# A two-layer decoder trunk on one core: the FFN's gate and up product as seven half-size products in place of eight

## The chip, the core and the metric

The kernel runs on one core of a Trainium2 chip: TensorE (PE) for matrix products, VectorE (DVE), ScalarE (ACT) and GpSimd (POOL) for elementwise work, SyncE (SP) for issuing transfers. The metric is the device time of one launch, in microseconds; lower is better.

## The reference

Two layers, each of them FFN, mixer, FFN, over 512 tokens of width 1024; the mixer of layer 0 is sparse attention over selected keys, that of layer 1 a gated spatial mixer. Only the FFN is touched by the change. It is run four times, with weights of its own each time:

```python
D_MODEL = 1024; SEQ = 512; D_FF = 2816
def swiglu(x, w_in, w_out):
    gate, up = jnp.split(x @ w_in, 2, axis=-1)
    return (jax.nn.silu(gate) * up) @ w_out
...
    h = x
    for i in range(DEPTH):
        h = h + 0.5 * swiglu(rmsnorm(h, norm_g[i, 0]), ffn_w_in[i, 0], ffn_w_out[i, 0])
        hn = rmsnorm(h, norm_g[i, 1])
        y = mixer_a(...) if kind == 0 else mixer_b(...)
        h = h + y
        h = h + 0.5 * swiglu(rmsnorm(h, norm_g[i, 2]), ffn_w_in[i, 1], ffn_w_out[i, 1])
    return rmsnorm(h, final_g)
```

## The kernel before

**Layout.** The residual stream stays in SBUF as eight tiles `H[j]` of 128 features x 512 tokens, features on the partitions. `weigh` (L177 to L180) turns each into two fp32r parts: `XH[j]` is the tile times the norm's gain, rounded, and `XL[j]` what the rounding left. The row scale of the norm is applied behind the product, since it depends on the token alone. Every weight tile of 128x128 is split in the same way into `whi` and `wlo`. `mul3` (L219 to L224) makes one product of full precision from three matmuls: whi by XH, whi by XL, wlo by XH, each with 512 columns. A product of one k tile is thus three matmuls and three weight loads.

**The weight stream.** All weights come in one order, written out by hand: `in_wst` holds them eight tiles to a load of 512 KB. `WeightStream` (L54) loads them on the SP queue into four `raw` buffers (L74), splits four tiles at a time (ACT makes `whi`, L91; DVE, in some stages POOL, makes `wlo`, L92) into six pairs of buffers, and `take` hands them to the next product. Each engine executes in the order in which the code is written, so a row that waits holds all rows behind it on its engine.

**The FFN** (`ffn`, L247). w_in has 22 gate tiles and 22 up tiles of output columns. The first four (gate 0, up 0, gate 1, up 1) are made together in four PSUM banks, k by k, in `group` (L230), so that they can start while the tiles of `XH` are still being made; all others one after the other, eight k each, in `single` (L240). `token_scale` (L198) makes the row scale with two matmuls against ones. `activate` (L256 to L268) multiplies gate and up by the row scale, applies silu and splits the result into `yh` and `yl`. When 11 of the 22 are there, their share of the product with w_out is made, and `scalar_tensor_tensor` at L318 adds half of it to `H[j]`. That is done twice; in the last FFN the second time in two halves of 256 tokens (`parts=2`), so that the final norm of one half can run beside the products of the other. `finish` starts the next stage's `weigh` and square sum as soon as a tile of `H` is complete. In the first FFN the `weigh` of tile k+1 and the square sum run in hooks behind k (`behind`), and a table of biases for the mixer, `dist`, is written to DRAM behind k = 3 (L345).

## Time and profile before

| what | value |
|---|---|
| median of 3 runs | 2143.5 us (2143.36 to 2143.62) |
| the profiled execution | 2143.43 us |
| its span, first to last instruction | 2141.7 us |
| PE busy | 2122.9 us, 9816 matmuls |
| PE weight loads busy | 1768.2 us |
| DVE busy | 1141.6 us |
| ACT busy | 752.7 us |
| POOL busy | 131.7 us |
| mean DMA rate | 100 GB/s |

Busy time is printed from the start of an instruction to its modelled end. Matmuls are pipelined: a matmul begins before the printed end of the one in front, and the distance between two starts tells what one costs in a row of them. An engine's share of the span is an average over stages; the rows by window and the timeline show a stage by itself.

### The profile page before, as it was taken

To read this page: it belongs to the slowest core of one execution; us is meant where nothing else is said; L and a number is where in the kernel's file an instruction comes from. 1 tells how busy PE (TensorE), PEld (TensorE's weight loads), DVE (VectorE), ACT (ScalarE), POOL (GpSimd) and SP (SyncE) were. 2 spreads that over 40 slices of the span, in tenths; PEclk is the share of its full clock that TensorE was granted. 3 is DMA by queue.
4 is the path that set the end of the run, shared out by engine and by line. 5 is a ranking of instruction groups with operands and counts; after the bars stand their busy time and mean duration, and the time that the engine had idled before them with its cause. 6 is when DMAs were issued, how large, how long until landed. Compare 5 with 4: busy or idle time off the path is not lost.

```text
span 2141.7 us, 25553 instructions
## 1 busy us (share of the span) xinstructions
PE 2122.9 (99%) x9816; PEld 1768.2 (83%) x9816; DVE 1141.6 (53%) x1968; ACT 752.7 (35%) x1317; POOL 131.7 (6%) x122
## 2 busy tenths in 40 slices
PE   8999999999999999999999999999999999999998
...
GB/s 182 134 99 99 94 93 99 88 105 83 61 89 99 98 99 93 95 88 108 99 98 93 95 99 89 149 88 90 97 91 94 86 89 104 99 99 94 94 127 129
DMA packets 60426, 214.67 MB, mean 100 GB/s; under 512 B 7232, under 2 KB 8320, under 8 KB 60176
## 3 DMA queue, kind: packets, MB, share of 16 engines
...
## 4 chain that ended last, share of the span: by engine, by line
PE 95%; DMA 3%; issue 1%; POOL 1%; DVE 0%; ACT 0%; POOLq 0%; ACTq 0%
PE acc L222 16%; PE acc L223 16%; PE acc L224 16%; PE aux L224 12%; PE aux L222 12%; PE aux L223 12%; DMA raw<-in_wst 2%; PE aux L648 1%; PE acc L647 1%; PE aux L647 1%; PE acc L648 1%; PE aux L646 1%; PE acc L646 1%; PE aux L698 1%; PE acc L565 1%
## 5 line engine op out<-in xcount | busy, mean ns | idle before, releaser
L91 ACT ACTIVATE whi<-raw 128x512 fp32r<-128x512 f32 x768 | 466.5, 625 | 743.6 <-PE acc L223 351.5
L92 DVE TENSOR_TENSOR wlo<-raw,whi 128x512 fp32r<-128x512 f32 x698 | 474.8, 701 | 445.4 <-ACT whi L91 445.1
L222 PE MATMUL acc<-xh,whi 128*128 128x512 f32 x1048 | 418.1, 399 | 6.4 <-ACT xh L179 5.5
L224 PE MATMUL acc<-xh,wlo 128*128 128x512 f32 x1048 | 409.0, 390 | 0.6 <-POOL wlo L92 0.6
L223 PE MATMUL acc<-xl,whi 128*128 128x512 f32 x1048 | 409.0, 390 | 0.0
L222 PE MATMUL aux<-xh,whi 128*128 128x512 f32 x720 | 280.2, 389 | 1.0 <-ACT whi L91 1.0
L224 PE MATMUL aux<-xh,wlo 128*128 128x512 f32 x720 | 280.2, 389 | 0.6 <-POOL wlo L92 0.6
L223 PE MATMUL aux<-xl,whi 128*128 128x512 f32 x720 | 280.1, 389 | 0.0
L222 PEld LDWEIGHTS acc<-xh,whi 128*128 128x128 f32 x1048 | 197.4, 188 | 49.0 <-ACT xh L179 5.5
L224 PEld LDWEIGHTS acc<-xh,wlo 128*128 128x128 f32 x1048 | 197.1, 188 | 42.5 <-POOL wlo L92 1.1
L223 PEld LDWEIGHTS acc<-xl,whi 128*128 128x128 f32 x1048 | 197.4, 188 | 41.9 <-issue 1.4
L222 PEld LDWEIGHTS aux<-xh,whi 128*128 128x128 f32 x720 | 135.1, 188 | 29.4 <-ACT whi L91 1.4
L224 PEld LDWEIGHTS aux<-xh,wlo 128*128 128x128 f32 x720 | 135.1, 188 | 29.2 <-POOL wlo L92 1.1
L223 PEld LDWEIGHTS aux<-xl,whi 128*128 128x128 f32 x720 | 135.1, 188 | 28.0
L222 PE MATMUL aux<-yh,whi 128*128 128x512 f32 (+1 forms) x396 | 144.8, 366 | 0.0
L222 PE MATMUL acc<-yh,whi 128*128 128x512 f32 (+1 forms) x396 | 144.8, 366 | 0.0
L223 PE MATMUL aux<-yl,whi 128*128 128x512 f32 (+1 forms) x396 | 144.7, 365 | 0.0
L224 PE MATMUL aux<-yh,wlo 128*128 128x512 f32 (+1 forms) x396 | 144.7, 365 | 0.0
L223 PE MATMUL acc<-yl,whi 128*128 128x512 f32 (+1 forms) x396 | 144.7, 365 | 0.0
L224 PE MATMUL acc<-yh,wlo 128*128 128x512 f32 (+1 forms) x396 | 144.7, 365 | 0.0
L92 POOL TENSOR_TENSOR wlo<-raw,whi 128x512 fp32r<-128x512 f32 x70 | 93.3, 1346 | 166.3 <-ACT whi L91 114.6
L245 DVE TENSOR_TENSOR yl<-a,yh 128x512 fp32r<-128x512 f32 x88 | 62.5, 711 | 61.5 <-ACT yh L244 61.5
...
## 6 DMA issues: line engine op xcount, KB each, us to landing
raw<-in_wst SPq DMA_DIRECT2D x383, 512.0 KB, 3.5
dist<-rows POOLq DMA_DIRECT2D x1, 2560.0 KB, 56.8
...
wT<-in_wspT POOLq DMA_DIRECT2D x1, 512.0 KB, 8.3
```

Source lines behind the costliest of these rows:

```text
L91: self.nc.scalar.activation(hi, src, AF.Copy)
L92: self.lo_engine.tensor_tensor(lo, src, hi.bitcast(F32), op=ALU.subtract)
L222: mm(ps, wh, xh, start=first, stop=False)
L223: mm(ps, wh, xl, start=False, stop=False)
L224: mm(ps, wl, xh, start=False, stop=last)
L245: nc.vector.tensor_tensor(lo, src, hi.bitcast(F32), op=ALU.subtract)
L565: mm(po[0][:, b * P:(b + 1) * P], V[j][:, h * P:(h + 1) * P], pT[:, j * P:(j + 1) * P], start=j == 0, stop=j == b)
L646: mm(banks[t], xh, wh, start=k == 0, stop=False)
L647: mm(banks[t], xl, wh, start=False, stop=False)
L648: mm(banks[t], xh, wl, start=False, stop=k == KD - 1)
L698: mm(ps[:, t * P:(t + 1) * P], V[t][:, d * P:(d + 1) * P], wT[:, g, :], start=True, stop=True)
```

## The change

Gate and up tiles 0 and 1 stay as they are, in `group`. The other 20 pairs are taken two at a time, ten double pairs for each FFN: two gate tiles and the two up tiles beside them. For such a double pair the sum over k is cut in two (even and odd k tiles) and the tokens in two (`n1`, the first 256, and `n2`). The product of a 2x2 arrangement of weights (gate and up by even and odd k) with a 2x2 arrangement of operands (even and odd k by first and second half) is then made with seven products in place of eight, by Winograd's form of Strassen's scheme.

- `sums(kp)` makes the four sums of operands that are needed, for each of four pairs of k tiles: ACT scales two tiles of `H` by the gain, POOL makes four differences, ACT and DVE split them into `TH[kp]` and `TL[kp]`. It is called in `group`'s hooks behind k = 1, 3, 5, 7.
- `_source` makes the weights of the seven products ("forms") from four loads r11, r21, r22, r12 (gate by even k, up by even k, up by odd k, gate by odd k): forms 0, 3 and 6 are loads as they are, forms 1, 2, 4 and 5 are DVE sums. Each form is eight weight tiles, and ACT and DVE split it in instructions of 1024 columns.
- `two_pairs` issues the seven products, each 2 x 4 x 3 matmuls of 256 columns, into three PSUM banks A, B, C. ACT copies intermediate results out of PSUM (m1, m5, u2, u3), DVE and POOL add them, POOL multiplies the gate by the row scale, and silu, the product and the split into `yl` are spread over the next products by `later` and `step`.
- `WeightStream` works in units of eight tiles in place of four. Plain units ("P") are split into three buffers `w`, forms ("F") into these or two more, `x`; forms are only made inside an FFN. Of the loads, r22 has a single buffer of its own.
- The output product is made in three chunks (3, 4 and 3 double pairs; 8, 8 and 6 k tiles) in place of two halves of 11, the first four `H` tiles together, the others one by one. In front of silu only the gate is multiplied by the row scale; for the up half it is applied here, times 1/2 (`rh`), so that `H[j]` takes two DVE instructions in place of one.
- The row scale is made from four columns (`scale_columns`, `scale_rows`) with fp32 matmuls. In the last stage the output is scaled in place in `H`, and each tile has a transfer of its own in place of one for two tiles.

```diff
+CHUNKS = (3, 4, 3)
+FFN_PLAN = "PPPP" + "SSS" + "P" * 8 + "SSSS" + "P" * 8 + "SSS" + "P" * 6
+PLAN = FFN_PLAN + "P" * 37 + FFN_PLAN + FFN_PLAN + "P" * 72 + FFN_PLAN + "P" * 6
+N_LOADS = sum(4 if k == "S" else 1 for k in PLAN)
...
+    RINGS = {"raw": 4, "r22": 1, "w": 3, "x": 2}
+    FORMS = 7
...
+                self.loads += [("raw", base + 4), ("raw", base + 4), ("r22", base + 6), ("raw", base + 5)]
+                self.units += [("F", n, f) for f in range(self.FORMS)]
...
+    def _free(self, ring, below):
+        used, n = self.used[ring], self.RINGS[ring]
+        return len(used) < n or used[-n] < below
...
+    def _split(self, src, hi, lo, s=slice(0, LOAD * P)):
+        self.nc.scalar.activation(hi[:, s], src[:, s], AF.Copy)
+        self.lo_engine.tensor_tensor(lo[:, s], src[:, s], hi[:, s].bitcast(F32), op=ALU.subtract)
...
+    def _source(self, i, f):
+        r11, r21, r22, r12 = (self.raw.get(i + j) for j in range(4))
+        tt = self.nc.vector.tensor_tensor
+        if f == 0:
+            return r11
+        if f == 1:
+            self.sum = self.spool.tile([P, LOAD * P], F32, tag="wsum", bufs=1, name=f"wsum{i}")
+            tt(self.sum, r21, r22, op=ALU.add)
+            return self.sum
+        if f == 2:
+            tt(self.sum, self.sum, r11, op=ALU.subtract)
+            return self.sum
+        if f == 3:
+            return r12
+        if f == 4:
+            tt(r21, r11, r21, op=ALU.subtract)
+            return r21
+        if f == 5:
+            tt(r12, r12, self.sum, op=ALU.subtract)
+            return r12
+        return r22
...
+            if kind == "F" and self.spool is None:
+                break
+            self._load_to(self.loaded + 4)
+            rings = [r for r in ("w", "x")[:1 if kind == "P" else 2] if self._free(r, self.current)]
+            if not rings:
+                break
+            src = self.raw[i] if kind == "P" else self._source(i, f)
+            hi, lo = self._parts(u, rings[0])
...
+    def scale_columns(ps):
+        for t in range(NT):
+            mm(ps[:, t:t + 1], acc[0][:, t * P:(t + 1) * P], ones[:, :1], start=True, stop=True)
+        v = small.tile([P, NT], F32, tag="vcol", bufs=1, name=uname("vcol"))
+        nc.vector.tensor_scalar(v, ps[:, :NT], 1.0 / D, EPS, op0=ALU.mult, op1=ALU.add)
+        return rsqrt(v, [P, NT])
+    def scale_rows(rc, ps):
+        for t in range(NT):
+            mm(ps[:, t * P:(t + 1) * P], rc[:, t:t + 1].broadcast_to([P, P]), ident, start=True, stop=True)
+        rb = small.tile([P, S], F32, tag="nwy512", bufs=1, name=uname("rb"))
+        rh = small.tile([P, S], F32, tag="ms", bufs=1, name=uname("rh"))
+        nc.scalar.activation(rb, ps, AF.Copy)
+        nc.scalar.activation(rh, ps, AF.Copy, scale=0.5)
+        return rb, rh
...
+            def sums(kp):
+                xg, t = gate_tile(), gate_tile()
+                for i in range(2):
+                    k = 2 * kp + i
+                    nc.scalar.activation(xg[:, i], H[k], AF.Copy, scale=g_sb[:, norm, k:k + 1])
+                tt = nc.gpsimd.tensor_tensor
+                tt(t[:, 0, n1], xg[:, 0, n2], xg[:, 0, n1], op=ALU.subtract)
+                tt(t[:, 0, n2], xg[:, 1, n2], xg[:, 0, n2], op=ALU.subtract)
+                tt(t[:, 1, n1], xg[:, 1, n2], t[:, 0, n1], op=ALU.subtract)
+                tt(t[:, 1, n2], xg[:, 1, n1], t[:, 1, n1], op=ALU.subtract)
+                split(t.rearrange("p a b -> p (a b)"), TH[kp].rearrange("p a b -> p (a b)"),
+                      TL[kp].rearrange("p a b -> p (a b)"))
+            def right(f, kp):
+                if f in (0, 3, 5):
+                    k, s = ((2 * kp, n1), (2 * kp + 1, n1), (2 * kp + 1, n2))[(0, 3, 5).index(f)]
+                    return XH[k][:, s], XL[k][:, s]
+                i = {1: 0, 4: 1, 2: 2, 6: 3}[f]
+                return TH[kp][:, i], TL[kp][:, i]
...
+            def plain_pairs(banks, g):
+                for i in range(2):
+                    nc.vector.tensor_tensor(g[:, i], banks[2 * i], R["b"], op=ALU.mult)
+                nc.scalar.activation(g, g, AF.Silu)
+                def up():
+                    for i in range(2):
+                        nc.vector.tensor_tensor(g[:, i], g[:, i], banks[2 * i + 1], op=ALU.mult)
+                later.append(up)
+                later.append(lambda: as_y(g))
+            def two_pairs(pair, tag, between=()):
+                A, B, C = bank(tag), bank(tag), bank(tag)
+                g = gate_tile()
+                specs = spec_pairs(pair)
+                copies = {}
+                def product(f, ps, first, last):
+                    wh, wl = W.form(f, specs)
+                    for p in range(2):
+                        for kp in range(KP):
+                            s = slice((p * KP + kp) * P, (p * KP + kp + 1) * P)
+                            mul3(ps[:, p * HALF:(p + 1) * HALF], (wh[:, s], wl[:, s]), right(f, kp),
+                                 first and kp == 0 and p == 0, last and kp == KP - 1, skip_group_check=True)
+                def copy(name, ps):
+                    copies[name] = fp.tile([P, S], F32, tag=name, bufs=1, name=uname(name))
+                    nc.scalar.activation(copies[name], ps, AF.Copy)
+                def halves(x):
+                    return x.rearrange("p (q n) -> p q n", n=HALF)
+                between = list(between)
+                def tick():
+                    if between:
+                        between.pop(0)()
+                    step()
+                product(0, A, True, True)
+                copy("m1", A)
+                tick()
+                product(1, C, True, True)
+                copy("m5", C)
+                tick()
+                product(2, A, False, True)
+                copy("u2", A)
+                tick()
+                product(3, B, True, True)
+                nc.vector.tensor_tensor(g[:, :, n1], halves(B), halves(copies["m1"]), op=ALU.add)
+                tick()
+                product(4, A, False, True)
+                copy("u3", A)
+                nc.gpsimd.tensor_tensor(copies["u3"], copies["u3"], copies["m5"], op=ALU.add)
+                tick()
+                product(5, C, False, True)
+                nc.vector.tensor_tensor(g[:, :, n2], halves(C), halves(copies["u2"]), op=ALU.add)
+                nc.gpsimd.tensor_tensor(g, g, R["b"].unsqueeze(1).broadcast_to([P, 2, S]), op=ALU.mult)
+                tick()
+                product(6, A, False, True)
+                flush()
+                def up():
+                    nc.vector.tensor_tensor(g[:, :, n1], g[:, :, n1], halves(A), op=ALU.mult)
+                    nc.vector.tensor_tensor(g[:, :, n2], g[:, :, n2], halves(copies["u3"]), op=ALU.mult)
+                later.append(lambda: nc.scalar.activation(g, g, AF.Silu))
+                later.append(up)
+                later.append(lambda: as_y(g))
...
+            banks = [bank() for _ in range(4)]
+            group(banks, [0, NJ, 1, NJ + 1], KD, spec_in,
+                  hooks={k: lambda k=k: (hooks[k]() if hooks else None, k == 3 and not hooks and scale(),
+                                         k == 5 and not hooks and spread(), k % 2 and sums(k // 2))
...
+            for ci, dps in enumerate(CHUNKS):
+                p0, Y[:] = done, []
+                done += 2 * dps
+                if ci == 0:
+                    done += 2
+                for i in range(dps):
+                    pair = 2 + 2 * n_dp
+                    between = ()
+                    if n_dp == 0:
+                        between = [scale, spread, lambda: plain_pairs(banks, g0)]
+                        between = between if hooks else between[2:]
+                    two_pairs(pair, "acc" if n_dp % 2 else "aux", between)
+                    n_dp += 1
...
+                    def add(j, ps):
+                        t = gate_tile()[:, 0]
+                        nc.vector.tensor_tensor(t[:, s], ps[:, s], R["h"][:, s], op=ALU.mult)
+                        nc.vector.tensor_tensor(H[j][:, s], H[j][:, s], t[:, s], op=ALU.add)
+                        if end:
                             finish(j, s)
+                    first = [bank(tag0) for _ in range(4)]
+                    group([ps[:, s] for ps in first], range(4), n_k, spec_out, y_parts)
+                    for j in range(4):
+                        add(j, first[j])
+                    for j in range(4, KD):
+                        ps = bank(tag1)
+                        single(ps[:, s], j, n_k, spec_out, y_parts)
+                        add(j, ps)
...
+        nc.scalar.activation(H[j][:, s], H[j][:, s], AF.Copy, scale=g_sb[:, 6, j:j + 1])
+        if s.start and j in (4, 5):
+            (norm_scale if j == 4 else norm_rest)(slice(0, s.start), False)
...
+            queue = nc.gpsimd if not end else nc.sync if j % 2 else nc.scalar
+            queue.dma_start(out[j, :, s], o)
...
```

The first of three places in which the order of instructions tells the change is ACT in the first FFN, from the `weigh` of tile 2 (`xh_82`) on; `sq` is the square, `gate` a scaled copy for `sums`, `th` the rounded part of the sums. Before:

```order
L179 ACTIVATE xh_82<-h_73,g_sb 128x512
L190 ACTIVATE sq_185<-h_72 128x512
L91 ACTIVATE whi_190<-raw_105 128x512
L91 ACTIVATE whi_194<-raw_109 128x512
L179 ACTIVATE xh_83<-h_74,g_sb 128x512
```

After:

```order
L282 ACTIVATE xh_82<-h_73,g_sb 128x512
L293 ACTIVATE sq_201<-h_72 128x512
L401 ACTIVATE gate_204<-h_71,g_sb 128x512
L401 ACTIVATE gate_204<-h_72,g_sb 128x512
L347 ACTIVATE th_139<-gate_205 128x1024
L121 ACTIVATE whi_214<-raw_109 128x512 x2
L121 ACTIVATE whi_222<-raw_113 128x1024
L282 ACTIVATE xh_83<-h_74,g_sb 128x512
```

The `weigh` of tile 3 now stands behind the first `sums`, whose `th` reads what POOL makes (`gate_205`).

The second place is ACT at the start of the second FFN, from the last `weigh` of the stage in front of it. Before (`ah` is the split of the square sum for `token_scale`):

```order
L179 ACTIVATE xh_87<-h_78,g_sb 128x512
L190 ACTIVATE sq_5302<-h_78 128x512
L91 ACTIVATE whi_5314<-raw_5199 128x512
L91 ACTIVATE whi_5332<-raw_5199 128x512
L91 ACTIVATE whi_5348<-raw_5240 128x512
L91 ACTIVATE whi_5366<-raw_5240 128x512
L201 ACTIVATE ah_5382<-sqacc_5112 128x512
```

After, the first two of four `sums` and what stands between them:

```order
L293 ACTIVATE sq_5835<-h_78 128x512
L121 ACTIVATE whi_5861<-raw_5695 128x1024
L401 ACTIVATE gate_5891<-h_71,g_sb 128x512
L401 ACTIVATE gate_5891<-h_72,g_sb 128x512
L347 ACTIVATE th_5844<-gate_5892 128x1024
L121 ACTIVATE whi_5901<-raw_5732 128x1024
L121 ACTIVATE whi_5907<-raw_5769 128x1024
L121 ACTIVATE whi_5913<-wsum_5911 128x1024
L401 ACTIVATE gate_5962<-h_73,g_sb 128x512
L401 ACTIVATE gate_5962<-h_74,g_sb 128x512
L347 ACTIVATE th_5845<-gate_5963 128x1024
L121 ACTIVATE whi_5973<-wsum_5911 128x1024
```

Between two calls of `sums` stand one plain split and the first forms, of which `whi_5913` reads a DVE sum.

The third place is DVE in the middle of a chunk. Before, one pair of tiles (`wlo` splits of four weight tiles, then the activation):

```order
L92 TENSOR_TENSOR wlo_1009<-raw_896,whi_1008 128x512
L92 TENSOR_TENSOR wlo_1027<-raw_896,whi_1026 128x512
L92 TENSOR_TENSOR wlo_1045<-raw_942,whi_1044 128x512
L92 TENSOR_TENSOR wlo_1063<-raw_942,whi_1062 128x512
L262 TENSOR_TENSOR gs_1078<-acc_960,nwy_398 128x512
L264 TENSOR_TENSOR us_1079<-acc_961,nwy_398 128x512
L265 TENSOR_TENSOR a_1081<-sg_1080,us_1079 128x512
L245 TENSOR_TENSOR yl_1087<-a_1081,yh_1086 128x512
```

After, from the first weight sum of a double pair to its fifth form:

```order
L140 TENSOR_TENSOR wsum_1765<-raw_1634,raw_1700 128x1024
L122 TENSOR_TENSOR wlo_1768<-wsum_1765,whi_1767 128x1024
L143 TENSOR_TENSOR wsum_1765<-wsum_1765,raw_1476 128x1024
L122 TENSOR_TENSOR wlo_1800<-wsum_1765,whi_1799 128x1024
L500 TENSOR_TENSOR gate_1628<-aux_1627,u_109_1730 128x2x256
L122 TENSOR_TENSOR wlo_1830<-raw_1702,whi_1829 128x1024
L148 TENSOR_TENSOR raw_1634<-raw_1476,raw_1634 128x1024
L122 TENSOR_TENSOR wlo_1863<-raw_1634,whi_1862 128x1024
L151 TENSOR_TENSOR raw_1702<-raw_1702,wsum_1765 128x1024
L122 TENSOR_TENSOR wlo_1897<-raw_1702,whi_1896 128x1024
```

Each sum is followed by the `wlo` that needs ACT's `whi` of that same sum.

## Rows read from the trace of the kernel before

**Rows 1.** The page's first part (busy us, share, instructions) and the chain's engines:

```profile
PE 2122.9 (99%) x9816; PEld 1768.2 (83%) x9816; DVE 1141.6 (53%) x1968; ACT 752.7 (35%) x1317; POOL 131.7 (6%) x122
PE 95%; DMA 3%; issue 1%; POOL 1%; DVE 0%; ACT 0%; POOLq 0%; ACTq 0%
```

**Rows 2.** Windows, 512-column and 256-column stretch; columns: stretch, length, busy by engine:

```profile
core 0: us, PE busy (x) PEld busy (x) DVE busy (x) ACT busy (x) POOL busy (x), PEclk, DMA share, GB/s
1050.00:1100.00 50.00, 50.00 (x222) 41.38 (x222) 23.19 (x36) 16.20 (x27) 0.00 (x0) 1.00 0.29 95
2070.00:2090.00 20.00, 20.00 (x169) 20.00 (x168) 12.95 (x24) 12.17 (x27) 0.00 (x0) 1.00 0.61 196
```

**Rows 3.** Timeline of PE: start us, us, instruction; 21 and 76 steps:

```profile
2059.62 0.39 PE L224 MATMUL acc<-xh,wlo 128*128 128x512 f32 x1
...
2064.38 0.39 PE L224 MATMUL acc<-xh,wlo 128*128 128x512 f32 x1
...
2120.02 0.28 PE L223 MATMUL acc<-yl,whi 128*128 128x256 f32 x1
...
2129.14 0.28 PE L224 MATMUL aux<-yh,wlo 128*128 128x256 f32 x1
```

**Rows 4.** Groups by line and shape: busy us, mean ns; last row min/median/max:

```profile
L92 DVE TENSOR_TENSOR wlo<-raw,whi 128x512 fp32r<-128x512 f32 x698 | 474.8, 701 | 445.4 <-ACT whi L91 445.1
L92 POOL TENSOR_TENSOR wlo<-raw,whi 128x512 fp32r<-128x512 f32 x70 | 93.3, 1346 | 166.3 <-ACT whi L91 114.6 <-DVE qs L434 36.1 <-PE acc L565 8.4
L262 DVE TENSOR_TENSOR gs<-acc,nwy 128x512 f32<-128x512 f32 x48 | 32.8, 684 | 0.0
L190 ACT ACTIVATE sq<-h 128x512 f32<-128x512 f32 x42 | 25.9, 618 | 5.9 <-POOL sqacc L191 5.9
L191 DVE TENSOR_TENSOR sqacc<-sqacc,sq 128x512 f32<-128x512 f32 x35 | 24.0, 685 | 0.0
L191 DVE TENSOR_TENSOR sqacc<-sqacc,sq 128x256 f32<-128x256 f32 x12 | 5.4, 448 | 6.4 <-ACT sq L190 6.4
L190 ACT ACTIVATE sq<-h 128x256 f32<-128x256 f32 x12 | 5.0, 418 | 21.2 <-DVE h L318 21.2
...
L803 POOL TENSOR_TENSOR hg<-hg,last_rb x11: 715/747/1199, 2106.9 to 2136.6; 128x256 f32<-128x256 f32 x11
```

**Rows 5.** Timeline of DVE beside POOL, early and in the mixer:

```profile
16.34 1.41 POOL L191 TENSOR_TENSOR sqacc<-sqacc,sq 128x512 f32<-128x512 f32 x1 [0.89 <-ACT sq L190]
16.52 1.78 DVE L180 SCALAR_TENSOR_TENSOR xl<-h,g_sb,xh 128x512 fp32r<-128x512 f32 x1
...
465.98 2.54 POOL L92 TENSOR_TENSOR wlo<-raw,whi 128x512 fp32r<-128x512 f32 x2 [3.31 <-ACT whi L91]
...
467.84 0.68 DVE L400 MATCH_REPLACE8 score<-m,score 128x512 f32<-128x512 f32 x1
```

**Rows 6.** Timeline of the first FFN: last `weigh`, first matmul behind `group`:

```profile
19.60 0.70 ACT L179 ACTIVATE xh<-h,g_sb 128x512 fp32r<-128x512 f32 x1
...
30.79 0.39 PE L222 MATMUL aux<-xh,whi 128*128 128x512 f32 x1
```

**Rows 7.** PE's waits (total, times, longest), first matmuls, slow windows, `dist` transfer:

```profile
PE acc L222 <- ACT xh L179: 5.5, 1, 5.5
PE aux L795 <- DVE nwy L171: 2.4, 1, 2.4
...
7.32 0.63 PE L222 MATMUL acc<-xh,whi 128*128 128x512 f32 x1
7.75 0.63 PE L223 MATMUL acc<-xl,whi 128*128 128x512 f32 x1
...
60.00:70.00 10.00, 9.51 (x42) 7.53 (x41) 3.05 (x4) 2.60 (x5) 3.00 (x2) 1.00 0.64 124
70.00:80.00 10.00, 7.36 (x29) 5.16 (x30) 3.86 (x5) 3.76 (x8) 4.92 (x4) 1.00 0.56 150
...
dist<-rows POOLq DMA_DIRECT2D x1, 2560.0 KB, 56.8
```

**Rows 8.** DMA issues of the weights: count, KB each, median us to landing:

```profile
raw<-in_wst SPq DMA_DIRECT2D x383, 512.0 KB, 3.5
```

320 lines of the change are left out of this document (179 added, 141 removed).

## The prediction

> **What bounds the kernel now.** I read the page's first part and chain first: TensorE (PE) is busy for 99% of the span and makes 95% of the chain of work that ended last [rows 1]. The windows tell what kind of busy: in an undisturbed 50 us PE starts 222 products with no idle time, while VectorE (DVE) works 23.2 us, ScalarE (ACT) 16.2 us and GpSimd (POOL) not at all [rows 2]. So the kernel is a queue of matmuls, and the price of one is its start-to-start time, not its printed duration, since printed durations overlap. In the timeline 21 steps of the 512-column form take 2059.62 to 2064.38, 0.2267 us each; 76 steps of the 256-column form take 2120.02 to 2129.14, 0.120 us each [rows 3]. Half the columns cost 0.53 of the time, not 0.50. PE loses time only at the very start: 5.5 us before the first product, ten products at half clock, and near 70 us, where weight loads crawl beside the 56.8 us transfer of the distance table [rows 7].
>
> **The change on PE.** Each of the four FFNs has ten double pairs in the new form. A double pair was 4 tiles x 8 k x 3 = 96 products of 512 columns, 96 x 0.2267 = 21.76 us. It becomes 7 products x 2 x 4 x 3 = 168 of 256 columns, 168 x 0.120 = 20.16 us. That is 1.60 us a pair, 64.1 us in forty; 7/8 on paper, 0.926 here. The last FFN's final pass, in 256-column halves, shrinks from 11 k to 6: 240 short products (28.8 us) become 120 long ones (27.2), another 1.6. **PE alone: -65.7 us.** That needs everything else hidden, and three things are not.
>
> The Trainium skill ("TensorE: Matmul & The Clock Gate", Back-to-back issue gap) gives columns / 2.4 GHz + 2.5 ns, so 0.109 us at 256 columns. The trace contradicts it at both sizes [rows 3]; by the page the pair would take 18.3 us by my estimate, some 73 us less in all than by the rows.
>
> **Prices of the new side work.** A DVE two-input operation takes 0.685 us at 512 columns and 0.448 at 256; an ACT one 0.618 and 0.418 [rows 4]. No 1024-column row exists. Carried on by the slope these are 1.16 for DVE (I take 1.2, since the weight split's own row is 0.70 at 512) and 1.02 for ACT. POOL takes 0.75 for 256 columns (the median of eleven) and 1.3 for 512 [rows 4]. POOL and DVE do not run two-input operations at the same time: a DVE operation that needs 0.7 took 1.78 and ended 0.55 behind the POOL operation it met, and the search operations with one tensor input kept 0.68 beside POOL [rows 5]. The Trainium skill ("GPSIMD Engine Reference", Key points) says that the two engines share SBUF interfaces and collide when the DVE instruction has two SBUF inputs; nearly all the new DVE work is of that kind. Without such collisions the third term below would be near nothing.
>
> **First loss: the operands' sums, FFNs two to four.** `sums(kp)` is called behind k = 1, 3, 5, 7. In ACT's order it is two scaled copies, and right behind them the split `th`, which waits for four chained POOL subtractions. ACT executes in order, so the weight splits behind `th` wait as well, and the next `sums` cannot start. One call: copies 1.4, POOL 4 x 0.75 + 0.2, `th` 1.0, so 5.7 us. Between the calls stand a weight split and the first forms: behind call one, wait for DVE's tl, two lo and wsum (4.7) and a hi (1.0); behind call two, tl, the next wsum and hi (3.5) and the two scale copies (1.1); behind call three a hi (1.0). Counted from PE's last product of the stage before, ACT is free at 3.2 us (it still has xh_7, its square and a split). 3.2 + 5.7 + 5.7 + 5.7 + 4.6 + 5.7 + 1 + 5.7 = 37.3, and DVE's part of the fourth sum is there at 38.6. PE wants it after its group (96 x 0.2267 = 21.8), the scale products (0.5), product 0 (2.9) and three triples of product 1 (1.1): 26.3. So PE stands 12.3 us, in two pieces. In rows 7 half clock costs ten products 0.43 instead of 0.23, 2 us; I add 2 for the long piece. **14.3 x 3 = +43 us** (15 to 48: as little as 5 each if copies or POOL overlap more with the end of the stage before, 16 with collisions on POOL). Before, the same place held one `ah` split, and PE showed no wait there: its longest beside the start's is 2.4 us, at the very end [rows 7].
>
> **Second loss: the first FFN.** The same calls stand between the splits of the operands themselves: in ACT's order xh_83 (k = 3) is now behind `th`, and xh_85 and xh_87 behind two more. The old trace has the last of the splits started at 19.6 and the group over at 30.8 us [rows 6]. Now: xh_82 ends near 10.8 us, square and copies 12.6, POOL (its square sum, then four) 16.2, th 17.2, three splits 19.2, xh_83 19.9: k = 3 waits 5.7 us. The second call also has the distance DMA and two square sums ahead of it on POOL: th 30.9, f0, the sum and f1 35.5, xh_85 36.1: k = 5 waits 10 us. The third likewise: xh_87 near 49.4, and the group ends near 55, 24.5 us later. The row scale behind product 1 waits for a 4-column rsqrt queued behind DVE's splits, 3.4. Half clock adds some 3 us more. What comes back: the old loss at 60 to 80 us, 4 and 17 products fewer than 46, 4.8 us [rows 7], because loads catch up meanwhile; a remainder of 1 stays, since r22 has one buffer. 24.5 + 3.4 + 3 + 1 - 4.8 = **+27 us** (10 to 35).
>
> **Third loss: DVE in the middle of a chunk.** Per pair DVE does, in order: four forms that are a sum, ACT's hi of it, then the lo (1.2 + 1.0 + 1.2 + 0.1 = 3.5, 14.0 together, and DVE stands idle during the hi because the lo is next in its queue); three plain lo, 3.6; the yl, 1.2; four operations on PSUM or gates at 0.68 [rows 4], 2.8. That is 21.6 us, 0.7 less where operations overlap as printed ones do: 20.9. POOL's two operations (1.3 and 2.6) fit into the 1.1 us gaps only in part and hold DVE 1.5 to 2.5 us; the single r22 buffer loads after the last lo and costs 0.9 beyond what covers it (3.5 us to land [rows 8] against 2.9). 23.7 against PE's 20.16: 3.5 us a pair too slow. Each chunk begins with forms split ahead during the output product. Walking the queue, the tightest form of a chunk's second pair is ready 4.0 us early (first chunk 1.9), the third 0.5, the fourth 3.1 late; first chunk's third, 1.6 late. 4.7 a FFN, **+19 us** (0 if POOL costs nothing; 38 at 25 us a pair).
>
> **What costs nothing.** Weight bytes are the same. ACT's share of a pair, nine operations of 1.02 and four copies of about 0.6, is 11.6 of 20 us. The `H` addition has two DVE operations in place of one; the next stage needs the last tile 19 us later. The mixers' double-length splits keep 24 pieces ahead as before; if that cover failed, one POOL split of 2.6 us would show. The tail is one short operation longer, 0.5 us, left out.
>
> **Sum.** -65.7 + 43 + 27 + 19 = +23. The profiled execution is 2143.43 us for a span of 2141.7, and the median is 2143.5, so no correction: 2166.
>
> **Rivals.** (a) Faster, the losses at the FFN starts are half as long: if the fourth `th` comes by 31 us in place of 37 (copies run while the stage before ends, POOL at 0.7) and DVE keeps up, the starts cost 35 in all: 2105 to 2139. It decides once the starts cost under 61 us together. For it: ACT is half idle [rows 2]; against: an engine in order cannot use that idle time. (b) Everything hidden: 2078 to 2085; against it stands the in-order wait itself. (c) Starts as computed, DVE keeps pace: +4, 2139 to 2148. (d) DVE at 25 us a pair or more, with starts at their upper bounds: 2190 to 2225. (e) The short product steps in half the long one's time, 0.1133: 168 x 0.1133 = 19.0 us a pair, -110 in all, with the same losses 2122; the 76 steps at 0.120 speak against it. The Trainium skill's gap, named above, points the same way and further.
>
> **Chances.** Forecast (2148 to 2190) 0.45; (a) 0.22; (b) 0.06; (c) 0.12; (d) 0.14; (e) 0.01. About 0.2% (4.3 us) is what a measurement can tell from no change, so (c) is "same". Faster (a), (b), (e) 0.29; slower 0.59. The bounds give -65.7 + 10 + 15 + 0 = -41 and -65.7 + 35 + 48 + 38 = +55; the range 2108 to 2200 leaves out (b), about half of (d) and the lowest edge of (a), some 0.15.
>
> **What would show it.** 256-column products step 0.120 us apart in runs without a wait. PE waits for `tl` or `th` in product 1 of each FFN, 8 to 14 us; for xh at k = 3, 5, 7 in the first. In the four-pair chunk DVE is busy or waiting on ACT throughout and PE waits for a `wlo` in the last pair. The forecast is wrong if PE's waits for `th` are under 5 us a FFN, or if DVE shows idle time that ends on PE in the fourth pair.

## The result, and the profile after

The changed kernel takes 2362.2 us (median of four runs, 2359.4 to 2364.6) against 2143.5 (2143.4 to 2143.6) on the same chip: 1.102 times as long, with a 95% interval of 1.100 to 1.104. That is 219 us more, where the prediction had 23. The direction was right and the size was far off; most of the 219 us comes from terms that the prediction had small or at nothing.

The page of the changed kernel, first part (busy us, share of the span, instructions) and the engines of the chain that ended last, answers to [rows 1]:

```profile
PE 2156.9 (91%) x12632; PEld 1921.4 (81%) x12632; DVE 1565.9 (66%) x1921; ACT 909.0 (38%) x1175; POOL 341.8 (14%) x227
...
PE 54%; DVE 23%; ACT 12%; issue 6%; POOL 3%; DMA 3%; ACTq 0%; SPq 0%; DVEq 0%; POOLq 0%
```

TensorE's share of the chain falls from 95% to 54%, and VectorE and ScalarE stand in it with 35% together. No engine but TensorE is busy for more than two thirds of the span, so no engine is short of time on average: the chain changes hands from engine to engine. PE's waits name the place (total us, times, longest; compare [rows 7]):

```profile
PE aux L325 <- ACT m L471: 46.8, 16, 3.2
PE acc L325 <- ACT m L471: 36.6, 12, 3.2
PE acc L325 <- ACT xh L282: 23.1, 4, 8.4
PE aux L325 <- ACT u L471: 21.6, 5, 9.0
```

The two costliest are not waits for a weight or an operand. `m` is ScalarE's copy of a product out of PSUM, which the next product into the same bank needs first. The timeline of one pair in the middle of a chunk (start us, us, instruction; in brackets the idle time before it and what ended it) shows how that copy comes so late:

```profile
1006.75 1.23 DVE L140 TENSOR_TENSOR wsum<-raw,raw 128x1024 f32<-128x1024 f32 x1 [1.56 <-DMA raw<-in_wst]
1009.71 1.84 POOL L497 TENSOR_TENSOR u<-u,m 128x512 f32<-128x512 f32 x1 [59.99 <-ACT u L471]
1010.44 2.20 DVE L143 TENSOR_TENSOR wsum<-wsum,raw 128x1024 f32<-128x1024 f32 x1
1015.73 3.31 POOL L501 TENSOR_TENSOR gate<-gate,rb 128x1024 f32<-128x1024 f32 x1 [4.17 <-DVE gate L500]
1016.70 3.42 DVE L148 TENSOR_TENSOR raw<-raw,raw 128x1024 f32<-128x1024 f32 x1
1018.57 0.28 PE L327 MATMUL aux<-th,wlo 128*128 128x256 f32 x1
1020.23 1.06 ACT L121 ACTIVATE whi<-raw 128x1024 fp32r<-128x1024 f32 x1 [5.50 <-DVE raw L148]
1021.20 0.58 ACT L471 ACTIVATE m<-aux 128x512 f32<-128x512 f32 x1
1021.83 0.39 PE L325 MATMUL aux<-th,whi 128*128 128x256 f32 x1 [2.98 <-ACT m L471]
1023.25 0.42 PE L325 MATMUL aux<-th,whi 128*128 128x256 f32 x1
1023.47 0.41 PE L326 MATMUL aux<-tl,whi 128*128 128x256 f32 x1
...
1032.30 1.22 DVE L140 TENSOR_TENSOR wsum<-raw,raw 128x1024 f32<-128x1024 f32 x1
```

Read it from below. PE stands from 1018.9 to 1021.8 for the copy `m`. The copy has no long work of its own (0.58 us), but in ScalarE's order it is behind `whi` of form 4, a form that is needed two products later. That `whi` has waited 5.5 us for VectorE's sum at L148, and the sum took 3.42 us in place of 1.2 because it met GpSimd's multiplication. The next pair's first sum starts 25.55 us behind this pair's. VectorE's loop is the clock, and TensorE is tied to it from a chunk's second pair on.

That is seen in TensorE's lost time, here and below the sum, over its matmuls in a stretch, of the distance between two starts less 0.2267 us (512 columns) or 0.120 (256). By pair in FFN 2, in us:

| chunk | 1st pair | 2nd | 3rd | 4th |
|---|---|---|---|---|
| first | 12.1 | 5.8 | 4.8 | |
| second | 0.0 | 4.7 | 6.1 | 4.6 |
| third | 0.0 | 5.1 | 6.1 | |

The other FFNs agree within 2 us. The 12.1 hold most of what the start of the FFN costs. The first pairs of the other two chunks lose nothing, since forms were split ahead during the output product; every pair behind them pays about the difference between 25.5 and 20.16 us.

The wait itself is not all that a pair loses. In the windows around it (stretch, length, busy by engine, granted clock, DMA) the clock is 0.66 of full for 5 us behind the wait, and products of 256 columns then start 0.21 us apart instead of 0.120:

```profile
1018.00:1022.00 4.00, 1.02 (x9) 0.82 (x8) 2.80 (x2) 1.77 (x3) 1.04 (x1) 1.00 0.18 40
1022.00:1027.00 5.00, 5.00 (x30) 5.00 (x31) 3.82 (x5) 3.71 (x5) 0.00 (x0) 0.66 0.18 73
1027.00:1032.00 5.00, 5.00 (x44) 5.00 (x43) 4.00 (x5) 2.11 (x3) 0.00 (x0) 1.00 0.52 187
```

By stage, cut at the start of the last `xh` of each stage (the split of the next stage's last operand), in us; four of the kernels of the experiments are set beside the two:

| stage | before | after | sums ahead | no operand sums | no new side work | best found |
|---|---|---|---|---|---|---|
| FFN 1 | 373.8 | 440.8 | 405.6 | 428.8 | 391.6 | 394.6 |
| mixer A | 256.9 | 259.2 | 260.3 | 259.2 | 260.2 | 260.7 |
| FFN 2 | 359.5 | 408.1 | 368.4 | 392.9 | 355.1 | 358.0 |
| FFN 3 | 359.5 | 406.2 | 366.6 | 392.6 | 355.1 | 357.0 |
| mixer B | 416.1 | 418.1 | 419.1 | 418.8 | 417.9 | 419.0 |
| FFN 4 and the end | 375.8 | 430.4 | 393.5 | 417.3 | 379.7 | 384.2 |

Nearly all the loss is in the four FFNs; the stages of the mixers are 2.3 and 2.0 us longer.

### The profile page after: what moved, and what is told of

Same layout as the page of the kernel before. It is cut to its first block, busy times and chain, and to the rows that moved or that the text cites. A ratio compares the mean times of both kernels' runs of the same rounds, so it can differ in the third digit from the quotient of the medians.

```text
span 2362.8 us, 30604 instructions
## 1 busy us (share of the span) xinstructions
PE 2156.9 (91%) x12632; PEld 1921.4 (81%) x12632; DVE 1565.9 (66%) x1921; ACT 909.0 (38%) x1175; POOL 341.8 (14%) x227
## 4 chain that ended last, share of the span: by engine, by line
PE 54%; DVE 23%; ACT 12%; issue 6%; POOL 3%; DMA 3%; ACTq 0%; SPq 0%; DVEq 0%; POOLq 0%
PE acc L325 9%; PE acc L327 9%; PE acc L326 8%; ACT whi L121 8%; DVE wlo L122 6%; PE aux L325 6%; PE aux L327 6%; PE aux L326 6%; DVE raw L148 5%; DVE wsum L143 3%; DMA raw<-in_wst 2%; DVE wsum L140 1%; DVE raw L151 1%; DVE h L563 1%; DVE gate L562 1%
## 5 line engine op out<-in xcount | busy, mean ns | idle before, releaser
L122 DVE TENSOR_TENSOR wlo<-raw,whi 128x1024 fp32r<-128x1024 f32 (+1 forms) x395 | 495.9, 1261 | 299.8 <-ACT whi L121 296.8
L121 ACT ACTIVATE whi<-raw 128x1024 fp32r<-128x1024 f32 (+1 forms) x422 | 438.7, 1046 | 613.3 <-DVE raw L148 221.5
L325 PE MATMUL acc<-xh,whi 128*128 128x256 f32 (+1 forms) x888 | 311.8, 351 | 29.0 <-ACT xh L282 23.1
L326 PE MATMUL acc<-xl,whi 128*128 128x256 f32 (+1 forms) x888 | 300.9, 339 | 4.1 <-DVE xl L283 4.1
L327 PE MATMUL acc<-xh,wlo 128*128 128x256 f32 (+1 forms) x888 | 300.1, 338 | 0.0
L325 PE MATMUL aux<-th,whi 128*128 128x256 f32 x640 | 200.6, 313 | 79.9 <-ACT m L471 46.8
L325 PE MATMUL acc<-th,whi 128*128 128x256 f32 x640 | 191.4, 299 | 42.0 <-ACT m L471 36.6
L326 PE MATMUL aux<-tl,whi 128*128 128x256 f32 x640 | 197.6, 309 | 2.5 <-DVE tl L348 2.4
L327 PE MATMUL aux<-th,wlo 128*128 128x256 f32 x640 | 197.2, 308 | 0.0
L326 PE MATMUL acc<-tl,whi 128*128 128x256 f32 x640 | 188.8, 295 | 0.0
```

The source lines that it names most:

```text
L121: self.nc.scalar.activation(hi[:, s], src[:, s], AF.Copy)
L122: self.lo_engine.tensor_tensor(lo[:, s], src[:, s], hi[:, s].bitcast(F32), op=ALU.subtract)
L325: mm(ps, wh, xh, start=first, stop=False, **kw)
L326: mm(ps, wh, xl, start=False, stop=False, **kw)
L327: mm(ps, wl, xh, start=False, stop=last, **kw)
```

## The experiments

The kernels named "before" beside these runs took 2143.5 to 2144.8 us. A single time is that of one run. The four runs of the changed kernel lie 5 us apart, so differences of that size between single runs tell nothing.

**What holds a pair.** Four kernels, each with one thing different from the changed kernel. The first moves only ScalarE's order: `copy` comes ahead of the splits of later forms, which `W.ahead()` then asks for.

```diff
                     nc.scalar.activation(copies[name], ps, AF.Copy)
+                    W.ahead()
```

> Edit: behind products 0, 1, 2 and 4 the copy out of PSUM is issued on ACT ahead of the splits of later forms, in place of behind them; nothing else moves. Theory A (VectorE's own queue sets the pair at 25.5 us: its work, its idle time on ACT's hi of a sum, collisions with POOL, the wait for a load): the pair stays near 25.5 us in the middle of a chunk, PE's waits for copies go, and others for whi and wlo come; PE only stops trailing the forms by two to three products, 6 to 8 us for each of 12 chunks: 2260 to 2300. Theory B (the copies behind the hi of form 4 are the loss, VectorE could keep up): a pair falls to about 20.2 us and the time to 2140 to 2180.

It took 2334.3 us, 28 less and above both ranges, though with the pair that A expected. Its waits (view as above) say why no more:

```profile
PE acc L328 <- ACT u L474: 44.0, 12, 4.1
```

The waits for `m` became waits for `u`, the later copies of a pair, which still stand behind the Silu and another sum's `whi`. A pair still takes 25.05 us (sums at 993.36 and 1018.41). In the four-pair chunk of FFN 2 TensorE now loses 0.0, 1.0, 7.4 and 4.2 us: the second pair is nearly freed, the third pays for it. To take the copies out of the queue is not enough while VectorE's loop is that long.

The second leaves GpSimd's two operations of each pair out.

```diff
-                nc.gpsimd.tensor_tensor(copies["u3"], copies["u3"], copies["m5"], op=ALU.add)
...
-                nc.gpsimd.tensor_tensor(g, g, R["b"].unsqueeze(1).broadcast_to([P, 2, S]), op=ALU.mult)
```

> Leaves out POOL's two operations of each double pair (the sum of u3 and m5, and the gate times the row scale). Theory A with collisions as the row reads (two DVE sums stretched from 1.2 to 2.2 and 3.4 us): the pair falls by about 3.2 us to 22.3, the time by 128 us to about 2235. Theory B, or collisions off the path: within 30 us of 2362.

2252.2 us, 110 less, or 2.75 us a pair; A said 128. In its timeline the two sums that had met GpSimd take their own time, and a pair takes 22.4 us (sums at L140 start at 959.08 and 981.46):

```profile
985.12 1.22 DVE L143 TENSOR_TENSOR wsum<-wsum,raw 128x1024 f32<-128x1024 f32 x1
...
990.34 1.22 DVE L148 TENSOR_TENSOR raw<-raw,raw 128x1024 f32<-128x1024 f32 x1
```

The third leaves the four sums of weights out.

```diff
-            tt(self.sum, r21, r22, op=ALU.add)
...
-            tt(self.sum, self.sum, r11, op=ALU.subtract)
...
-            tt(r21, r11, r21, op=ALU.subtract)
...
-            tt(r12, r12, self.sum, op=ALU.subtract)
...
+        return (r11, r21, r21, r12, r21, r12, r22)[f]
```

> Leaves out the four sums of weights: forms 1, 2, 4 and 5 are split from plain loads. Theory A: VectorE has 4.8 us of sums and 4.8 us of idle time on ACT less for each pair, PE becomes the bound at 20.2 to 20.5 us a pair, and the time falls to 2140 to 2165, which is the cost of the FFN starts and little else above the products. Theory B: the copies stand behind a hi that now waits for nothing late, so the time falls as well; the two differ in the other runs, not in this one. If a third cost of the middle is there (the 256-column products slower than 0.120 us, PSUM), 2200 or more.

2187.2 us, 175 less, above the range that was expected by some 20. Behind the first pair of an FFN no pair loses time, except in the first FFN beside the transfer of the distance table. GpSimd's operations are all there in this kernel, so by themselves they cost TensorE nothing like 110 us: they cost it through the sums.

The fourth has all the work, in another order. VectorE issues the sums of forms 2 and 4 ahead of form 1's `wlo` and that of form 5 ahead of form 4's (`between` below), so that ScalarE's `whi` of a sum never waits for one that was only just asked for.

```diff
         self.nc.scalar.activation(hi[:, s], src[:, s], AF.Copy)
+        if between:
+            between()
         self.lo_engine.tensor_tensor(lo[:, s], src[:, s], hi[:, s].bitcast(F32), op=ALU.subtract)
```

> Same work; the sums for forms 2, 4 and 5 are issued on VectorE ahead of the lo of the form before, so that ACT can make their hi meanwhile (form 2's sum is written into r11 for that). Theory A: three idle times of 1.2 us go, 3.6 us a pair, and the hi of form 4 in front of the copy m1 is there early: 21.9 us or less a pair, 2190 to 2230. Theory B: the copy is free since the hi of form 4 waits for nothing late: about 20.2 us a pair and 2150 to 2170.

2215.5 us, 147 less and in A's range, with no instruction removed. Its timeline of VectorE in a pair, and a window of 20 us of such a pair:

```profile
839.79 1.22 DVE L140 TENSOR_TENSOR wsum<-raw,raw 128x1024 f32<-128x1024 f32 x1
841.04 1.22 DVE L149 TENSOR_TENSOR raw<-raw,raw 128x1024 f32<-128x1024 f32 x1
842.30 1.23 DVE L150 TENSOR_TENSOR raw<-wsum,raw 128x1024 f32<-128x1024 f32 x1
...
848.67 3.31 DVE L152 TENSOR_TENSOR raw<-raw,raw 128x1024 f32<-128x1024 f32 x1
...
860.60 1.22 DVE L140 TENSOR_TENSOR wsum<-raw,raw 128x1024 f32<-128x1024 f32 x1
```

```profile
825.00:845.00 20.00, 20.00 (x169) 20.00 (x169) 17.59 (x15) 10.58 (x13) 5.27 (x2) 1.00 0.30 106
```

The three sums stand in a row without the 1.2 us in which VectorE used to wait for ScalarE behind each. The collision with GpSimd is still there (3.31 us at L152) and costs nothing now: VectorE's first sums of this pair and the next are 20.8 us apart, TensorE starts 169 products in 20 us, as many as in [rows 2], and in FFN 2 the nine pairs behind the first lose 1.3 us together in place of 37.2. Its lost time from 714 to 1034 us is 11.2, most of it where the FFN ends. **So the pairs were lost to the order of VectorE's queue.** The collisions lengthened a loop that was too long already.

**What the starts cost.** In the changed kernel the sums of the operands (`sums`, with `th` and `tl`) were left out.

```diff
-                                         k == 5 and not hooks and spread(), k % 2 and sums(k // 2))
+                                         k == 5 and not hooks and spread(), None)
...
-                return TH[kp][:, i], TL[kp][:, i]
+                return XH[k][:, s], XL[k][:, s]
```

> The changed kernel with the sums of operands left out (the four scaled copies, GpSimd subtractions and splits th and tl at the start of every FFN; products 1, 2, 4 and 6 read plain halves of the operands instead, so the output is not the reference's). Nothing else differs, so it prices the first and second loss of the prediction, 43 + 27 = 70 us, together. Theory P (they are a cost of their own): 2280 to 2300. Theory Q (VectorE's loop in the chunk behind it sets the time anyway and gives the gain back): 2320 to 2350.

2311.3 us, 51 less, between the two theories' ranges. By the table (profiled spans, 53 apart) it is 15.2, 13.6 and 13.1 us in FFNs 2, 3 and 4, 42 together, and 11.9 in the first; so the sums are a cost of their own in the later FFNs, as P has it, and something gives much of it back in the first. There the last operand is split at 33.4 us in place of 51.6, and TensorE meets another wall sooner, in the first pairs (PE's waits from 60 to 130 us, where the changed kernel's longest was 9.0):

```profile
PE aux L325 <- ACT u L472: 16.6, 1, 16.6
```

Can order alone give it back? On the kernel with the sums ahead, `th` and `tl` were issued a step later than the GpSimd subtractions that they wait for: `behind_sums` issues the split of one sum, and then the copies and subtractions of the next.

```diff
-                                         k == 5 and not hooks and spread(), k % 2 and sums(k // 2))
+                                         k == 5 and not hooks and spread(), behind_sums(k))
```

> The kernel with the weight sums issued ahead (2215.5 us), and the split of the operand sums (th, tl) issued one step behind the GpSimd subtractions that it waits for, so that ScalarE has other work in between; in the first FFN two tiles later. Theory S (the FFN starts are lost because ScalarE stands at th behind GpSimd; by TensorE's steps the start of the second FFN still costs 12 us, the first one 25 to 30): 2145 to 2175, the first FFN's group ends near 40 us in place of 60. Theory T (the starts are bound by the amount of work on ScalarE, VectorE and GpSimd, not by the order): 2205 to 2220.

2204.4 us, 11 less: at the lower edge of T, far from S. ScalarE's wait at `th` does go in the first three sums, and the last operand of the first FFN is split at 39.3 us instead of 49.9. Other waits take its place, in the same 60 us:

```profile
32.71 0.80 PE L325 MATMUL acc<-xl,whi 128*128 128x512 f32 x1 [4.17 <-DVE xl L282]
...
48.17 1.06 ACT L346 ACTIVATE th<-gate 128x1024 fp32r<-128x1024 f32 x1 [3.38 <-POOL gate L407]
```

VectorE's `xl` is now late, since its operations and GpSimd's meet (its 1.2 us operations take 1.6 to 1.75 between 24 and 31 us). And the four sums share two buffers, so that each still waits for the one before.

**What is left with neither.** Operand sums, weight sums and GpSimd's two operations of a pair were all left out of the changed kernel together, as in the three runs above.

> The changed kernel with all its new side work left out: no sums of operands, no sums of weights, neither GpSimd operation of a pair (the output is not the reference's). What stays is TensorE's work, the splits and the new output pass. Theory L (the prediction's three losses are all there is): 2078 to 2090. Theory H (the hand-over behind a last chunk of only six tiles of k, where VectorE needs 4.8 us a tile and TensorE 4.1, and the rsqrt columns are losses of their own, 9 us at each of two hand-overs and some 15 at rsqrt and the end): 2105 to 2120.

2161.4 us: above both ranges. TensorE's products alone give 2143.5 - 65.7 = 2078, so some 84 us have nothing to do with the sums or with GpSimd's two operations. In the pairs of FFN 2 TensorE loses nothing (690 to 960 us: 0.0). The losses stand at two kinds of place. One is the first two pairs of the first FFN. The wait there (PE's waits from 40 to 130 us), ScalarE's wait for the weights behind it, and the transfers issued from 20 to 100 us (count, KB, median us to landing):

```profile
PE acc L307 <- ACT m L454: 16.5, 1, 16.5
```

```profile
80.00 2.00 ACT L121 ACTIVATE whi<-raw 128x1024 fp32r<-128x1024 f32 x2 [23.40 <-DMA raw<-in_wst]
```

```profile
raw<-in_wst SPq DMA_DIRECT2D x9, 512.0 KB, 14.9
dist<-rows POOLq DMA_DIRECT2D x1, 2560.0 KB, 55.2
```

While the distance table is written, weights land in 14.9 us instead of 3.5 [rows 8]. That alone is not the loss: before the change, loads issued from 22.9 to 58.1 us, beside the same transfer, landed 20 to 31 us later, and TensorE lost only 4.2 us. But five of them were issued by 49.9 us and landed one every 7.7 us from 46.5 on. Without side work one load is issued at 25.9, the next not before 49.2, and that one lands at 72.5. The waits in the SP queue from 20 to 90 us, the kind with the longest wait of each, before and without side work (total, times, longest), show the difference:

```profile
SPq L74 <- DMA raw<-in_wst: 22.2, 5, 7.6
SPq L103 <- DVE wlo L122: 46.6, 3, 22.9
```

Counted in the order of the loads, the one that waited 22.9 us is r22 of the second pair, whose single buffer the first pair's r22 still held. In the changed kernel the queue stood still longer, 41.7 us, for a `raw` buffer that VectorE's sum at L148 was to free. So loads are asked for too late to ride out the transfer. What a second buffer would give back was not tried.

The other kind is the end of an FFN. The timeline of the changed kernel there, VectorE from one of the last four output columns to the next, and TensorE at the start of FFN 3:

```profile
1093.59 0.68 DVE L562 TENSOR_TENSOR gate<-acc,rh 128x512 f32<-128x512 f32 x1
1094.31 0.69 DVE L563 TENSOR_TENSOR h<-h,gate 128x512 f32<-128x512 f32 x1
1095.79 0.75 DVE L283 SCALAR_TENSOR_TENSOR xl<-h,g_sb,xh 128x512 fp32r<-128x512 f32 x1 [0.79 <-ACT xh L282]
1096.46 0.68 DVE L294 TENSOR_TENSOR sqacc<-sqacc,sq 128x512 f32<-128x512 f32 x1
1097.26 1.23 DVE L122 TENSOR_TENSOR wlo<-raw,whi 128x1024 fp32r<-128x1024 f32 x1
1098.40 0.68 DVE L562 TENSOR_TENSOR gate<-acc,rh 128x512 f32<-128x512 f32 x1
...
1103.95 0.50 PE L325 MATMUL acc<-xh,whi 128*128 128x512 f32 x1 [3.59 <-DVE gate L562]
1107.42 0.79 PE L325 MATMUL acc<-xh,whi 128*128 128x512 f32 x1 [2.35 <-DVE gate L562]
```

A column takes VectorE 4.81 us; TensorE makes one of the last four in 18 x 0.2267 = 4.1 us (six tiles of k), and the four columns ahead of them ended together. So VectorE falls behind, and the next stage stands at a bank that VectorE has not read. Three runs on the kernel with the sums ahead take this apart. First a longer last pass:

```diff
-CHUNKS = (3, 4, 3)
+CHUNKS = (3, 3, 4)
```

> The kernel with the weight sums issued ahead (2215.5 us), and the chunks of an FFN as 3, 3, 4 double pairs in place of 3, 4, 3: the last output pass then has 8 tiles of k instead of 6, so 5.4 us of TensorE for each of its last four columns instead of 4.1. Theory H (TensorE stands at the hand-over of FFN 2 to 3 and 3 to mixer B, and at the end, because VectorE's chain per tile, 4.8 us with the additional operation, is longer than 4.1 us): 10 less at each hand-over and 5 less at the end, 2 to 3 more for the longer half-column pass: 2190 to 2205, no wait for the gate tile longer than 1 us. Theory K (the banks are taken in an order that no longer fits): 2210 to 2220, the same waits.

2198.9 us, 16.5 less. H holds; one wait of 2.4 us at a gate tile stays. Next, other banks for the stage behind, and the scale of mixer A asked for later:

```diff
+        ACC, AUX = ("aux", "acc") if (layer, which) == (1, 0) else ("acc", "aux")
...
-            banks = [bank() for _ in range(4)]
+            banks = [bank(ACC) for _ in range(4)]
...
-            group([kw] + pq, ["kw"] + [QI0 + P * i for i in range(4)], KD, spec_a, hooks={1: scale})
+            group([kw] + pq, ["kw"] + [QI0 + P * i for i in range(4)], KD, spec_a, hooks={5: scale})
```

> The kernel with the weight sums ahead (2215.5 us), and in the third FFN the two sets of PSUM banks exchanged, so that the stage behind each output pass starts in banks other than the ones of the last four output columns; in mixer A the row scale is asked for at the sixth step instead of the second. Nothing is taken off any engine. Theory H2 (the hand-over is lost because the next stage accumulates at once into banks that VectorE has not read yet, 11 us at two places, and at mixer A because of the early scale, 9 us): 2180 to 2190, and the waits for the gate tile vanish. Theory H1 (VectorE's backlog itself reaches TensorE; other banks only move the wait to the operands): 2205 to 2216.

2214.2 us, 1 less: H2 falls. The waits for the gate tile are gone, and in FFN 3's group TensorE waits for the row scale instead, which stands in VectorE's queue behind the last columns, a `tl` that waits 3.94 us for `th`, and the weight sums:

```profile
PE acc L360 <- DVE nwy L273: 10.9, 1, 10.9
```

Last, the addition as one operation, as it was before the change:

```diff
-                        nc.vector.tensor_tensor(t[:, s], ps[:, s], R["h"][:, s], op=ALU.mult)
-                        nc.vector.tensor_tensor(H[j][:, s], H[j][:, s], t[:, s], op=ALU.add)
+                        nc.vector.scalar_tensor_tensor(H[j][:, s], ps[:, s], 0.5, H[j][:, s], op0=ALU.mult, op1=ALU.add)
```

> The kernel with the weight sums ahead (2215.5 us), and the addition to the residual as one VectorE operation (a constant half of the bank plus the old value) as before the change, in place of two; the multiplication by the row scale is left out, so the output is not the reference's. VectorE's chain per output column falls from 4.8 to some 4.1 us, beside TensorE's 4.1. Theory H1 (VectorE's backlog in the last pass of each FFN, made by the second operation on top of a pass of six tiles): 2195 to 2203, 3 to 5 us at each of the four ends of an FFN. Theory H3 (the backlog is that of the four columns that end together, whatever the operation): 2210 to 2215.

2191.8 us, 24 less and more than H1 said, for an operation of 0.69 us in each column. VectorE's step from column to column is now 4.09 us, TensorE's own:

```profile
1014.17 0.68 DVE L560 SCALAR_TENSOR_TENSOR h<-acc,h 128x512 f32<-128x512 f32 x1
...
1018.26 0.68 DVE L560 SCALAR_TENSOR_TENSOR h<-acc,h 128x512 f32<-128x512 f32 x1
```

**Whether the pieces add up.** Sums ahead, late split and chunks of 3, 3, 4 together:

> Weight sums ahead, late split and chunks of 3, 3, 4 together. If the three losses are separate the gains add: 2125 to 2160, by S and H; by T and K 2205 to 2220.

2190.3 us (four runs), 1.022 times before (1.020 to 1.024), between the two ranges. It is 25 less than the sums ahead alone, where 11 and 16.5 make 27.5: the gains add, but the one of the late split was not the expected one. Then three smaller moves on top of this kernel (the transfer behind the first chunk, the row scale's transposes behind product 0, the first half's norm a tile later), and with them the copies of the first run:

```diff
-        nc.gpsimd.dma_start(d, rows.unsqueeze(1).broadcast_to([HEADS, P, TBW]))
...
+                if ci == 0 and middle:
+                    middle()
...
-                        between = between if hooks else between[2:]
+                        between = between if hooks else [spread, lambda: None, between[2]]
...
-        if s.start and j in (4, 5):
+        if s.start and j in (4, 6):
```

> All work in place: weight sums ahead, late split, chunks 3, 3, 4 (2190 us), and further the row scale's transposes moved from the sixth step of the group behind product 0, the distance table's transfer issued behind the first chunk instead of at 28 us, and the norm of the first half one tile later at the end. If the waits seen at these places (4 us at rsqrt in each FFN, 11 us in the first pair beside the transfer, 5 at the end) are losses of their own: 2155 to 2170. If they only move: 2180 to 2195.

> The same with ScalarE's copies out of PSUM ahead of the splits of later forms. Under the reading that the weight sums ahead have already unlocked the pairs, the copies matter only in the first pair of an FFN (3.5 us each): 5 to 15 below the kernel without it. If the copies still held every pair: 30 below or more.

2199.3 and 2200.3 us, 9 and 10 more than without the moves, where the worse of the two readings was 2180 to 2195 for the first and a gain of 5 to 15 was expected of the second. The waits move and grow, and the copies first give nothing once the sums are ahead. With the transfer behind the first chunk TensorE's lost time in the first pair falls from 14 to 3 us, and from 130 to 180 us it rises from nothing to 17. The row scale's 4 us became as long a wait for `th`. The next two runs drop these moves. Both have the 2190 us kernel with the exchanged banks and the later scale of mixer A, and cut the transfer in eight pieces; the first of them also gives the temporaries of the operand sums other buffers and moves the row scale's transposes to the last step of the group:

```diff
+                      lambda h=h: nc.gpsimd.dma_start(d[h:h + 1], rows[h:h + 1].unsqueeze(1).broadcast_to([1, P, TBW]))
...
-                xg, t = gate_tile(), gate_tile()
+                xg, t = (v.bitcast(F32) for v in y_tiles())
```

> All work in place: weight sums ahead, late split, chunks 3, 3, 4 (2190 us), the banks and the scale of the run before, the distance table's transfer in eight pieces spread over the second to fourth pair, the temporaries of the operand sums in the still empty output tiles (so that the four sums don't wait for each other), and the row scale's transposes at the last step of the group. By the waits at these places (7 at each of two hand-overs, 3 at mixer A, 12 beside the transfer, 8 at each of three FFN starts): 2135 to 2150. If the starts are bound by ScalarE and VectorE's work: 2160 to 2170.

> The kernel of the run before without the temporaries in the output tiles and with the transposes where they were: starts as at 2190 us. Theory D (the 12 us beside the transfer come from one burst that outlasts the loads' lead): 2158 to 2168, no wait over 4 us in the first pair. Theory E (they come from the bytes, wherever they fall): 2170 to 2180, the same wait in later pairs.

2216.5 us (four runs, 1.033 times before, 1.032 to 1.035) and 2233.6, far above every range that was named. The pieces are a loss: in the second kernel TensorE loses 23 us from 62 to 130 and 27 from 130 to 180. The rows on transfers of the second, over the whole run:

```profile
raw<-in_wst SPq DMA_DIRECT2D x380, 512.0 KB, 3.3
dist<-rows POOLq DMA_DIRECT2D x8, 320.0 KB, 27.8
```

A piece has an eighth of the bytes and takes half as long as the whole, but not by itself: the first took 14.1 us, the last, with others still in flight, 47.6. Together some piece is under way for 98 us in place of 55, so the time in which weights land late has grown. Neither D nor E said that. The last run has the other buffers and the transfer in one piece, at its old place:

> The run with all pieces (2216.5 us) with the distance table's transfer in one piece at its old place. If the transfer's eight pieces alone cost the first FFN its 42 us there (438 to the last operand against 395), and the temporaries in the output tiles give 6 us in each later FFN: 2168 to 2178. If the temporaries cost the first FFN something too: 2180 to 2195.

2175.5 us, as expected: the fastest kernel with the new form, and 41 less than with the pieces. Its FFNs 2 and 3 take 358.0 and 357.0 us, 1.5 and 2.5 less than before the change. The first FFN, the end and the mixers are 21, 8 and 7 more. No version beat the kernel before.

## Why the prediction was right or wrong, point by point

| term | predicted | measured | from |
|---|---|---|---|
| TensorE's products alone | -65.7 | -65.7 | worked out from steps of 0.120 and 0.2267; no lost time in the pairs of FFNs 2 to 4 without side work |
| starts of FFN 2 to 4 | +43 | +42 | after against no operand sums |
| start of FFN 1 | +27 | +12 | the same |
| VectorE in a chunk | +19 | +150 | no operand sums against no side work |
| everything else | 0 | +84 | no side work against 2078 |
| sum | +23 | +222 | the profiled spans are 221 apart |

The measured column adds up by construction, since each row is what the next thing left out gave back and 84 is the rest. The prices hold in that order only: without the weight sums (2187.2 us) the operand sums and GpSimd's two operations together cost 26 us (2187.2 against 2161.4), not 54 for the operand sums alone.

**TensorE's products: right.** The 256-column steps are 0.120 us wherever TensorE does not wait and its clock is full, as [rows 3] had them, and nearly all of the gain of 16 us an FFN is there once nothing holds it: FFN 2 without side work is 4.4 us shorter, with 10.3 us lost in it, most of them at its end. The formula that the prediction sets against [rows 3] is given in the Trainium skill ("TensorE: Matmul & The Clock Gate", Back-to-back issue gap) as the gap of an isolated matmul. For a stream of weight loads and matmuls, as here, the section has other figures, so the 18.3 us are not what it says of such a stream.

**First loss: right in size, not in place.** 15.2, 13.6 and 13.1 us against 14.3. But the forecast wanted 8 to 14 us of it at `tl` or `th` in product 1 and called itself wrong under 5 us at `th`; PE stands there 3.2 to 4.5 us, and with `tl` 3.9 to 5.4. The rest is at `nwy`, at a `u` in the first pair and in steps at half clock. The size also needs the weight sums between the calls, which the walk had counted in. Without them FFNs 2 to 4 are only 5.4 to 6.4 us longer than without any side work.

**Second loss: right on the order, wrong on what comes back.** The last `xh` was put near 49.4 us and came at 51.6; the waits at k = 3, 5 and 7 are 3.8, 8.4 and 5.4 us, and the group ends at 59.7 us where 55 was forecast. The steps that failed are the 4.8 us that were to come back "because loads catch up meanwhile" and the 1 us for r22's single buffer. The transfer that cost 4.2 us before costs 9 us in one wait now and 17 without the operand sums, and a group that ends earlier only meets it earlier. So +12 is what the operand sums add to a stretch that the late loads would hold anyway.

**Third loss: the step that failed most.** "Walking the queue, the tightest form of a chunk's second pair is ready 4.0 us early" took a form split in time as enough, and had the leads cover three pairs of a four-pair chunk. They cover the first alone: the second already loses 4.7 us. A product also needs its bank, the bank needs ScalarE's copy, and in ScalarE's order the copy stands behind the `whi` of a form that comes later, so a lead in forms is lost on it. The run with the copies first prices that at 28 us. The larger part is the pace: 23.7 us a pair was forecast and 25.5 came, 5.4 more than TensorE's in place of 3.5, as GpSimd's two operations hold VectorE 1.0 and 2.2 us and the load 1.56; and the leads are too short for it even with the copies out of the way (0.0, 1.0, 7.4 and 4.2 us). Why the walk had them so much longer is not taken apart further. Even the bound of 38 us, made with 25 us a pair, kept the leads in it, so the true 150 lay outside the range. The prediction named the 1.0 us hi in which "DVE stands idle" and added it up; that a different order of the same operations removes it, and with it nearly the whole loss, it did not see.

GpSimd and VectorE excluding each other was right, and from [rows 5]. With 1.22 us alone, a sum took 2.20 beside 1.84 and 3.42 beside 3.31, ending 1.08 us behind the other each time. The Trainium skill ("SBUF — State Buffer", SBUF: two separate sides) calls the shared ports an exclusive lock for the whole instruction, with the loser fully blocked; these rows agree. The run without GpSimd's operations prices it at 110 us in the queue as it was, and in the run with the sums ahead the pairs lose almost nothing beside the same collisions.

**"What costs nothing": wrong on the `H` addition.** The second operation was covered by "the next stage needs the last tile 19 us later". That looked at when an operand is needed, not at how fast VectorE gets through eight columns: the pass had shrunk from eleven to six tiles of k, from 7.5 us a column to 4.1, below VectorE's 4.8. In the kernel with the sums ahead the second operation costs 24 us over the four ends, and the longer pass alone gives 16.5 back.

Of the 84 us, a term that the prediction put at nothing, the traces place some 16 beside the transfer, 7 in the first group, 11 and 11 and 11 behind FFNs 1 to 3, 20 at the end and 2 in mixer B, by TensorE's lost time with that of before taken off. The remaining 6 are not placed.

**The rivals.** (d), a loop of 25 us or more with starts at their upper bounds, had half of its condition met: the loop took 25.5 us, but the starts cost 42 and 12, not 48 and 35. It came nearest at 2190 to 2225, with a chance of 0.14, and missed by 137 us since it priced the loop at 38. (a), (b) and (c) needed a VectorE that keeps pace; the sums ahead gave that, and still took 2215.5 us, for the starts and ends.
